# An emission planner with new costs, a margin for background row products, and bias tables loaded in three pieces

## The chip, the cores and the metric

The kernel runs on one core of one Trainium2 chip. The metric is the device time of one execution in microseconds; 1758.64 us is the median of three runs of the kernel before. The core's engines are TensorE (PE: matrix multiplies and transposes; PEld: the loading of its weights), VectorE (DVE), ScalarE (ACT), GpSimd (POOL) and SyncE (SP, which issues most transfers). Each runs its own queue of instructions in order and meets the others through semaphores.

## The reference

Two layers of a diffusion backbone, fp32, on 256 latent tokens and 256 context tokens of width 2048. What matters here, shortened:

```python
for i in range(2):
    shift, scale, gate = split(silu(c) @ ada_w[i] + ada_b[i], 3)        # modulation, 3 x 2048
    h = rms_norm(x, norm_g[i]) * (1 + scale) + shift
    if i == 0:
        y = na_ssd_mixer(h, hc, ...)      # hc: the context, modulated in the same way by c_ctx
    else:
        y = short_conv_mixer(h, ...)      # h @ w_in, gated convolution over 3 tokens, @ w_out
    x = x + gate * y

# in na_ssd_mixer: one projection h @ w_in (14400 columns), then
s_lat = einsum(q, k) * scale + bias       # 16 heads of 128; bias from the table rpb by (row, column) distance
s_lat = where(mask, s_lat, -inf)          # 16 columns' neighbourhood on a grid of 4 rows x 64
p = softmax(concat([s_lat, s_ctx]))
# beside them 32 state-space heads (8 groups), both directions; both parts @ w_out
```

## The kernel before

All matrix weights stream from HBM once, as tiles of 128 x 1024 fp32 (512 KB). Each is split into a high part (rounded to TensorE's fp32r format by ScalarE, line 420, `split`) and a low part (the fp32 tile minus the high part, by VectorE, line 427, `low_part`). A product is three passes: high by high, high by low, low by high. There are five raw buffers and three places for split weights (`w`), so the next weight's split waits until TensorE has left a place. `chunk` takes one split weight and issues its multiplies; `proj` runs over a column block. The first layer's 16 modulated row blocks are built in `ada_gen`; then come, block by block, q, k, gates, v, and the state-space inputs; then `w_out`, and the second layer.

Everything beside the weight products is written as generators: attention heads (`head_gen`), state-space groups (`group_gen`, `make_x`, `make_b`, `make_c`), norms of q and k (`kq_gen`), and the rest of the modulation as row products (`gemv_gen`): the gate of layer one and all of layer two, 128 tiles `adaT` of 128 x 1024, each multiplied by the broadcast vector `csb` and summed by one VectorE instruction (line 823, `gp`). A generator yields what it needs before its next step, as `W_(engine, tiles, nb)`, and the kernel writes out its instructions when the planner allows the step.

The planner (`Plan`) is a model of the chip that runs while the program is written. It keeps a clock per engine (`t`), the planned end of the last write (`w`) and the last read (`r`) of each tile part, and one DMA clock at 270 bytes a nanosecond. `add` books each emitted instruction with `cost`. After each few multiplies `pump` asks `may` for each waiting step, in three queues with horizons: `urgent` 4500 ns, `side` (heads and groups) 2500 ns, `back` (the row products only) 1500 ns. For VectorE and ScalarE the test is

```python
return t <= now + hor and rdy <= max(t, now) + 400     # line 270; now: PE's clock, t: the engine's
```

where `rdy` is the planned end of the writes that the step needs. For a step of TensorE in `back`, 4000 ns are added to `rdy`. So the planner sets no time on the chip: it sets only the order in which each engine's instructions stand in its queue. `force` writes out steps until a condition holds; line 1888 forces the row products of the second layer before its norm, line 1723 the last ones.

The attention bias of a head is a tile `bias` of 128 x 768, two of them in turn. Each head loads 672 columns of it (line 1073) with one transfer; the host builds the table with two gaps of 176 zeros between the parts that hold values (0 to 127, 304 to 367, 544 to 671). The mask is added to the three parts (line 1078), and the score step reads 2 x 208 columns, gaps included, for each half of the tokens (line 1096).

Of the kernel before, what the change touches and what calls it, by code (L numbers as in the profile page):

```python
# [37 lines left out]
class Plan:  # L38
# [5 lines left out]
    def __init__(self):  # L44
        self.t = dict.fromkeys(("PE", "DVE", "ACT", "POOL", "SP"), 0.0)
        self.w, self.r, self.last = defaultdict(float), defaultdict(float), defaultdict(float)
        self.dma = 0.0
        self.pool = (0.0, 0.0)

# [8 lines left out]
        hi = ap.offset + sum(abs(s) * (c - 1) for s, c in a)  # L58
        return [(n, u) for u in range(ap.offset // 256, hi // 256 + 1)]

    def ready(self, aps):
        return max((self.w[k] for a in aps for k in self.keys(a)), default=0.0)

    @staticmethod
    def size(a):
# [5 lines left out]
    def cost(self, e, op, i, ins, outs):  # L71
        n = max(self.size(a) for a in ins + outs)
        if e == "PE":
            n, cols = self.size(outs[0]), outs[0].ap[0][1]
            if i.is_transpose:
                return n / 1.2 + 3, 190
            if ins[0].dtype == F32R:
                return 9 + 0.434 * n, 190
            return 2 * max(55, n / 1.2) * (0.27 if cols == 32 else 0.52 if cols == 64 else 1) + (80 if cols < 128 else 0), 190
        if e == "DVE":  # L80
            if op == "Memset":
                return n * 0.26 + 60, 90
            if op in ("Reciprocal", "TensorReduce"):
                return n * 1.04 + 70, 90
            if len([a for a in ins if self.size(a) >= n]) >= 2 or op == "ISA" or self.psum(ins):
                return n * 1.22 + 70, 90
            return n * 0.6 + 130, 90
        if e == "ACT":
            return n * 0.85 + 150 + (200 if len(outs) > 1 else 0), 100
        if e == "POOL":  # L90
            return (n * 186 if n < 70 else n * 2.4) + 150, 60
        return 60, 0
# [5 lines left out]
    def add(self, b):  # L98
        i = b.ins
        e, op = self.NAMES[str(i.engine).split(".")[-1]], i.opcode  # L100
        ins = [x.bass_ap for x in i.ins if hasattr(x, "bass_ap")]
        outs = [x.bass_ap for x in i.outs if hasattr(x, "bass_ap")]
        ki, ko = [k for a in ins for k in self.keys(a)], [k for a in outs for k in self.keys(a)]
        s = self.t[e]
        for k in ki:
            s = max(s, self.w[k] + 60)
        for k in ko:
            s = max(s, 0.0 if e == "PE" else self.w[k] + 60, self.r[k] + 60)
        if op == "DMACopy":
            n = 4  # L110
            for _, c in outs[0].ap:
                n *= c
            self.t[e] = s + 450
            if e == "SP":
                self.dma = max(self.dma, s + 1000) + n / self.RATE
                done = free = self.dma + 1000
            else:
                done = free = max(self.dma, s + 1000) + n / self.RATE + 2500
        else:
            d, lat = self.cost(e, op, i, ins, outs)  # L120
            if e == "DVE" and not self.psum(ins + outs) and self.pool[0] <= s < self.pool[1]:
                s = self.pool[1]
            if e == "POOL":
                self.pool = (s, s + d)
            self.t[e] = s + d
            free, done = s + d, s + d + lat
        for k in ki:
            self.r[k] = max(self.r[k], free)
            self.last[k[0]] = max(self.last[k[0]], free)
        for k in ko:  # L130
            self.w[k] = done
            self.last[k[0]] = max(self.last[k[0]], done)
        return b

# [7 lines left out]
def kernel(ctx: ExitStack, tc, x, cx, ada0, w0, adaT, w_in, w_out, sc_in, sc_out, rpb, small, const,  # L142
# [7 lines left out]
    V, S, G, T, DMA = nc.vector, nc.scalar, nc.gpsimd, nc.tensor, nc.sync  # L150
    DMA2 = nc.scalar
    plan = Plan()
    E = plan.add

    def st(shape, tag, dt=F32, name=None):
        return sb.tile(list(shape), dt, tag=tag, name=name or tag, bufs=1)

    def drt(shape, name):
        return dr.tile(list(shape), F32, name="dram_" + name)
# [79 lines left out]
    def grow(task):  # L239
        _, t, h = task.cond  # L240
        if t - task.tmps > budget[0] or h - task.halves > budget[1]:
            return False
        cap(task, t, h)
        return True

    def may(task, hor, isurg):
        eng, aps, nb = task.cond
        if eng == "if":
            return aps()
        if eng == "grow":  # L250
            return grow(task)
        if nb and len(free_b) < nb + (0 if isurg else reserve[0]):
            return False
        if eng == "DVE":
            lows_try()
        now, t = plan.t["PE"], plan.t["ACT" if eng == "AQ" else eng]
        rdy = plan.ready(aps)
        if eng == "AQ":
            return t <= now + hor and rdy <= t
        if hor < 2000 and nb and sorted(plan.last[b.tensor.name] for b in free_b)[nb - 1] + 3000 > now:  # L260
            return False
        if hor < 2000:
            rdy += 4000 if eng == "PE" else 0
        if eng == "PE":
            if nb:
                rdy = max(rdy, sorted(plan.last[b.tensor.name] for b in free_b)[nb - 1])
            return rdy + (0 if isurg else 800) <= now + 100
        if eng == "SP":
            return rdy <= max(t, now) + 200
        return t <= now + hor and rdy <= max(t, now) + 400  # L270
# [7 lines left out]
    def pump():  # L278
        splits_try()
        again = True  # L280
        while again:
            again = False
            for q, hor in HOR[:2] if hold[0] else HOR:
                for task in list(q):
                    if not begin(task):
                        continue
                    if task.cond == "end":
                        sweep(q)
                        continue
                    if may(task, hor, q is urgent):  # L290
                        run(q, task)
                        if task.cond == "end":
                            sweep(q)
                        again = True
                        break
                if again:
                    break
# [134 lines left out]
    def lows_try():  # L432
        while lows and not hold[0] and plan.ready([lows[0][1]]) <= max(plan.t["PE"], plan.t["DVE"]) + 200:
            low_part()
# [340 lines left out]
    bias = [st([128, 3, 256], f"bias{k}") for k in range(2)]  # L775
# [149 lines left out]


    vd = drt([256, 512], "vd")
    dcol = P_("dcol")


# [136 lines left out]
    def head_gen(a, h):  # L1067
        hd = 4 * a + h
# [1 line left out]
        yield when(lambda: hd < 2 or ("pv", hd - 2) in got)  # L1070
        yield W_("SP")
        bf = bt.rearrange("p a b -> p (a b)")[:, :672]
        E(DMA.dma_start(bf, rpb[hd]))
        yield W_("DVE", bt)
        for o_, m_ in ((0, mask[:, 0:32]), (304, mid), (544, mask[:, 32:64])):
            n_ = m_.shape[-1]
# [77 lines left out]
        for i, (kt, vt, q_) in enumerate(BLOCKS):  # L1154
# [8 lines left out]
                          op=ALU.mult))  # L1163
# [388 lines left out]
    for h in range(4):  # L1552
        spawn(side, head_gen(0, h))
# [11 lines left out]
    def do_qk(a, nxt):  # L1565
        psQ = banks(2)
        proj(512, "act", psQ, 4)
        spawn(urgent, kq_gen("Q", a, psQ, 2, statq, QT, QL, True), 2)
        psK = banks(4)
        proj(512, "act", psK, nxt)  # L1570
        spawn(urgent, kq_gen("K", a, psK, 4, statk, KT, KL, True), 4)
        for h in range(4 if a < 3 else 0):
            spawn(side, head_gen(a, h))
# [19 lines left out]
    for h in range(4):  # L1593
        spawn(side, head_gen(3, h))
# [31 lines left out]
    done = []  # L1626
# [484 lines left out]
```

## Time and profile before

| | |
|---|---|
| median of 3 runs | 1758.64 us (1757.49 to 1760.16) |
| the profiled execution | 1761.34 us, of which the span of its instructions 1759.6 us |
| busy TensorE / VectorE / ScalarE | 1733.2 / 1218.6 / 768.1 us |
| mean granted TensorE clock | 0.999 |
| moved by DMA | 381.86 MB, 217 GB/s in the mean |

In the rows shown below, `L427` is line 427 of the kernel; `bank<-hH,w` names the tile written and the tiles read; a bracket `[0.77 <-DVE w L427]` is the idle time of the engine just before the instruction and what ended it. Rows of the timeline begin with the start in us from the span's start and the duration in us. `DVE raw L823 <- DMA raw<-in_adaT: 23.0, 24, 2.8` in the waits means: line 823 on VectorE waited for that transfer, 23.0 us in total, 24 times, 2.8 at most. In the table by stage each row is a stretch of time: its length, busy time and instruction count of each engine, the granted clock as a share of full speed, the busy share of the DMA engines, and GB/s. A transfer's row has its count, KB each, and the median us from issue to landing. TensorE's ends are modelled, so its busy time is not its peak rate.

### The profile page before, as it was taken

To read this page: it belongs to the slowest core of one execution; us is meant where nothing else is said; L and a number is where in the kernel's file an instruction comes from. 1 tells how busy PE (TensorE), PEld (TensorE's weight loads), DVE (VectorE), ACT (ScalarE), POOL (GpSimd) and SP (SyncE) were. 2 spreads that over 40 slices of the span, in tenths; PEclk is the share of its full clock that TensorE was granted. 3 is DMA by queue.
4 is the path that set the end of the run, shared out by engine and by line. 5 is a ranking of instruction groups with operands and counts; after the bars stand their busy time and mean duration, and the time that the engine had idled before them with its cause. 6 is when DMAs were issued, how large, how long until landed. Compare 5 with 4: busy or idle time off the path is not lost.

```text
span 1759.6 us, 25036 instructions
## 1 busy us (share of the span) xinstructions
PE 1733.2 (99%) x9451; PEld 1462.6 (83%) x9451; DVE 1218.6 (69%) x2042; ACT 768.1 (44%) x1330; POOL 31.4 (2%) x26
## 2 busy tenths in 40 slices
PE   6999999999999999999999999999999999999998
PEld 4777989888888888888888898888888888888887
DVE  5666777878476868676878687887668555555554
ACT  5333544446243436243436343664445444444432
POOL 0000100000000001000000000000000000000000
PEclk9999999999999999999999999999999999999999
DMA  9977644685765766665677567767867666666563
GB/s 368 347 295 258 206 150 150 201 241 190 231 198 158 239 190 209 207 220 171 212 219 219 180 213 239 242 227 266 290 218 251 208 187 192 191 191 191 190 205 120
DMA packets 188761, 381.86 MB, mean 217 GB/s; under 512 B 15536, under 2 KB 51168, under 8 KB 188640
## 3 DMA queue, kind: packets, MB, share of 16 engines
q1 hardware_dynamic: 181376, 373.68, 65.4%
q10 hardware_dynamic: 7264, 6.58, 1.1%
q8 instruction: 74, 1.21, 0.3%
q14 instruction: 47, 0.39, 0.1%
HBM read 372.71 MB, written 7.50 MB: 216 GB/s over the span
## 4 chain that ended last, share of the span: by engine, by line
PE 94%; DMA 2%; DVE 2%; ACT 1%; issue 0%; SPq 0%; POOL 0%; DVEq 0%; ACTq 0%
PE bank L195 90%; PE bank L199 3%; DMA tmp<-dram_csr 1%; DVE w L427 1%; DMA raw<-in_adaT 1%; DMA raw<-in_ada 0%; DVE raw L823 0%; DMA bias<-in_rpb 0%; ACT w L420 0%; DVE tmp L1456 0%; ACT tmp L1441 0%; DVE tmp L1445 0%; SPq L583 0%; ACT tmp L1451 0%; DVE tmp L759 0%
## 5 line engine op out<-in xcount | busy, mean ns | idle before, releaser
L420 ACT CAST w<-raw 128x1024 fp32r<-128x1024 f32 x343 | 359.1, 1049 | 519.9 <-PE bank L195 443.6
L427 DVE TENSOR_TENSOR w<-raw,w 128x1024 fp32r<-128x1024 f32 x343 | 416.5, 1218 | 232.9 <-ACT w L420 223.6
L195 PE MATMUL bank<-hH,w 128*128 128x256 f32 (+1 forms) x2064 | 488.4, 325 | 5.4 <-DVE w L427 5.4
L195 PE MATMUL bank<-w,hH 128*128 128x512 f32 x1280 | 406.3, 395 | 2.7 <-ACT hH L757 2.5
L195 PEld LDWEIGHTS bank<-hH,w 128*128 128x128 f32 x2064 | 345.7, 189 | 38.4 <-DVE w L427 6.6
L195 PE MATMUL bank<-hL,w 128*128 128x256 f32 (+1 forms) x1040 | 335.0, 322 | 0.0
L195 PEld LDWEIGHTS bank<-w,hH 128*128 128x128 f32 x1280 | 236.8, 188 | 54.1 <-issue 3.9
L195 PE MATMUL bank<-w,hL 128*128 128x512 f32 x640 | 249.5, 390 | 0.1
L195 PEld LDWEIGHTS bank<-hL,w 128*128 128x128 f32 x1040 | 197.0, 189 | 14.4
L195 PE MATMUL bank<-w,h 128*128 128x512 f32 x768 | 179.7, 390 | 0.0
L823 DVE CUSTOM_DVE_ANT_0 raw<-raw,csb 128x1024 f32<-128x1024 f32 x128 | 155.6, 1220 | 28.7 <-DMA raw<-in_adaT 23.0
L195 PEld LDWEIGHTS bank<-w,h 128*128 128x128 f32 x768 | 143.6, 188 | 29.6
L195 PEld LDWEIGHTS bank<-w,hL 128*128 128x128 f32 x640 | 120.1, 188 | 25.5 <-DVE hL L763 0.6
L195 PE MATMUL bank<-w,mix 128*128 128x512 f32 x588 | 138.6, 392 | 0.8 <-DVE w L427 0.8
L195 PEld LDWEIGHTS bank<-w,mix 128*128 128x128 f32 x588 | 109.3, 188 | 23.5 <-DVE w L427 1.7
L1276 DVE SCALAR_TENSOR_TENSOR tmp<-bank,cwh,tmp 128x508 f32<-128x508 f32 (+1 forms) x96 | 71.2, 745 | 1.8
L195 PE MATMUL bank<-KL,h 128*128 128x512 f32 x264 | 63.8, 389 | 0.0
L427 DVE TENSOR_TENSOR KL<-raw,KL 128x1024 fp32r<-128x1024 f32 x32 | 39.2, 1224 | 32.4 <-ACT KL L420 32.4
L427 DVE TENSOR_TENSOR QL<-raw,QT 128x1024 fp32r<-128x1024 f32 x32 | 39.2, 1224 | 29.4 <-ACT QT L420 29.3
L427 DVE TENSOR_TENSOR wL<-raw,wH 128x1024 fp32r<-128x1024 f32 x31 | 37.9, 1224 | 30.4 <-ACT wH L420 30.4
L195 PEld LDWEIGHTS bank<-KL,h 128*128 128x128 f32 x264 | 49.5, 188 | 10.2
L195 PE MATMUL bank<-QT,h 128*128 128x512 f32 x168 | 56.2, 391 | 0.0
(292 smaller groups left out, 1972.6 us busy)
## 6 DMA issues: line engine op xcount, KB each, us to landing
raw<-in_w_in SPq DMA_DIRECT2D x196, 512.0 KB, 3.8
raw<-in_adaT SPq DMA_DIRECT2D x128, 512.0 KB, 4.7
raw<-in_sc_in SPq DMA_DIRECT2D x128, 512.0 KB, 3.7
raw<-in_w_out SPq DMA_DIRECT2D x64, 512.0 KB, 4.9
raw<-in_ada SPq DMA_DIRECT2D x34, 512.0 KB, 6.7
raw<-in_sc_out SPq DMA_DIRECT2D x32, 512.0 KB, 3.6
PT<-in_ada SPq DMA_DIRECT2D x16, 512.0 KB, 6.9
raw<-in_w SPq DMA_DIRECT2D x16, 512.0 KB, 6.2
```

Of the source, the lines that this page charges most:

```text
L195: E(T.matmul(o, l, r, start=start, stop=stop, skip_group_check=True))
L199: E(T.transpose(o, i, ident if k == 128 else ident[:k, :k]))
L420: E(S.copy(H, v))
L427: E(V.tensor_tensor(out=Lo, in0=v, in1=H.bitcast(F32), op=ALU.subtract))
L823: E(V.tensor_tensor_reduce(out=raw, in0=raw, in1=csb, scale=1.0, scalar=0.0, op0=ALU.mult, op1=ALU.add, accum_out=gp[:, h, m:m + 1]))
L1276: E(V.scalar_tensor_tensor(out=do, in0=di, scalar=cwh[:, 32 * k + ch:32 * k + ch + 1], in1=do, op0=ALU.mult, op1=ALU.add))
```

## The change

Three edits.

1. The host's bias table has no gaps any more (320 columns). The two bias tiles' columns 128 to 543 are zeroed once by GpSimd, and each head loads its three parts with three transfers.
2. For a VectorE step of the `back` queue 2000 ns are added to `rdy`.
3. The planner's model: new costs of VectorE and ScalarE, a new latency to other engines, and no wait between instructions of the same engine (the planner keeps which engine wrote and read a part last).

```diff
@@ class Plan
+        self.wby, self.rby = defaultdict(str), defaultdict(str)
...
-    def ready(self, aps):
-        return max((self.w[k] for a in aps for k in self.keys(a)), default=0.0)
+    def ready(self, aps, e=None):
+        return max((self.w[k] for a in aps for k in self.keys(a) if self.wby[k] != e), default=0.0)
...
@@ def cost
+        wide = len([a for a in ins if self.size(a) >= n])
         if e == "DVE":
             if op == "Memset":
-                return n * 0.26 + 60, 90
+                return n * 0.26 + 60, 120
             if op in ("Reciprocal", "TensorReduce"):
-                return n * 1.04 + 70, 90
-            if len([a for a in ins if self.size(a) >= n]) >= 2 or op == "ISA" or self.psum(ins):
-                return n * 1.22 + 70, 90
-            return n * 0.6 + 130, 90
+                return n * 1.04 + 190, 120
+            if wide >= 2 or op == "ISA" or self.psum(ins):
+                return n * 1.045 + (137 if op == "ISA" else 128 if op == "TensorScalarPtr" else 70), 120
+            return (n * 0.4 + 205 if n > 32 else 80), 120
         if e == "ACT":
-            return n * 0.85 + 150 + (200 if len(outs) > 1 else 0), 100
+            if op == "Activation":
+                d = n * 0.83 + (110 if self.psum(ins) else 190 if len(outs) > 1 else 105)
+                return (d if self.psum(ins) else max(d, 293)), 120
+            return (n * 0.83 + 55 if self.psum(ins) else n * 0.85 + 90), 120
...
@@ def add
         for k in ki:
-            s = max(s, self.w[k] + 60)
+            if self.wby[k] != e:
+                s = max(s, self.w[k] + 60)
         for k in ko:
-            s = max(s, 0.0 if e == "PE" else self.w[k] + 60, self.r[k] + 60)
+            if self.wby[k] != e:
+                s = max(s, self.w[k] + 60)
+            if self.rby[k] != e:
+                s = max(s, self.r[k] + 60)
...
+        if op == "DMACopy":
+            e = "DMA"
         for k in ki:
+            if free >= self.r[k]:
+                self.rby[k] = e
             self.r[k] = max(self.r[k], free)
...
         for k in ko:
-            self.w[k] = done
+            self.w[k], self.wby[k] = done, e
...
@@ def may
-        rdy = plan.ready(aps)
+        rdy = plan.ready(aps, eng)
...
         if hor < 2000:
-            rdy += 4000 if eng == "PE" else 0
+            rdy += 4000 if eng == "PE" else 2000 if eng == "DVE" else 0
...
@@ before the first heads
+    for b_ in bias:
+        E(G.memset(b_.rearrange("p a b -> p (a b)")[:, 128:544], 0.0))
...
@@ def head_gen
-        E(DMA.dma_start(bf, rpb[hd]))
+        for o_, c_, n_ in ((0, 0, 128), (304, 128, 64), (544, 192, 128)):
+            E(DMA.dma_start(bf[:, o_:o_ + n_], rpb[hd, :, c_:c_ + n_]))
...
@@ on the host
-    gap = np.zeros((16, 128, 176), np.float32)
-    table = np.concatenate([pick(0, kc[:32]), gap, pick(0, kc[32:40]), pick(1, kc[24:32]), gap, pick(1, kc[32:])], axis=2)
+    table = np.concatenate([pick(0, kc[:32]), pick(0, kc[32:40]), pick(1, kc[24:32]), pick(1, kc[32:])], axis=2)
```

In a row such as `n * 1.045 + 70, 120`, `n` is the number of columns, the first value the time in ns until the engine is free, the second the time after that until another engine can use the result.

## The prediction

> **What bounds the kernel now.** I read the page's first two parts, then the chain of waits, the table by stage, the waits of TensorE, and the timeline around each of its waits.
>
> ```profile
> span 1759.6 us, 25036 instructions
> PE 1733.2 (99%) x9451; PEld 1462.6 (83%) x9451; DVE 1218.6 (69%) x2042; ACT 768.1 (44%) x1330; POOL 31.4 (2%) x26
> ```
>
> TensorE is busy in 1733.2 of 1759.6 us. The change touches none of its instructions, only their order and what they wait for. So the change can gain at most TensorE's idle time and what its clock lost. The table by stage tells where that lies (columns: busy us and instruction count of PE, PEld, DVE, ACT, POOL; then the granted clock, DMA share, GB/s):
>
> ```profile
> 0.00:40.00 40.00, 25.25 (x189) 16.79 (x189) 22.82 (x69) 24.97 (x55) 2.41 (x8) 1.00 0.96 373
> 200.00:240.00 40.00, 40.00 (x313) 38.48 (x312) 34.10 (x49) 25.57 (x55) 5.46 (x2) 1.00 0.63 196
> 400.00:440.00 40.00, 38.35 (x296) 35.65 (x293) 35.85 (x82) 23.57 (x65) 4.40 (x3) 1.00 0.57 182
> 640.00:680.00 40.00, 38.32 (x242) 33.90 (x240) 28.26 (x63) 24.16 (x75) 0.00 (x0) 1.00 0.74 226
> 680.00:720.00 40.00, 37.91 (x225) 33.45 (x226) 34.41 (x75) 16.83 (x34) 6.14 (x3) 0.96 0.47 147
> 1120.00:1160.00 40.00, 39.22 (x204) 32.37 (x203) 33.95 (x71) 23.78 (x48) 0.70 (x1) 1.00 0.82 258
> 1720.00:1760.00 40.00, 34.59 (x153) 28.31 (x151) 15.61 (x17) 7.70 (x8) 0.00 (x0) 0.98 0.32 105
> ```
>
> The first row's 14.75 us idle are the first transfers and norms; the last row's 5 us are the last multiply, add and store. No edit aims at either. Between them, TensorE waits five times on the low part of a weight (line 427: the fp32 weight minus its rounded copy, on VectorE):
>
> ```profile
> PE bank L195 <- DVE w L427: 6.2, 5, 3.0
> 409.53 0.50 PE L195 MATMUL bank<-hH,w 128*128 128x256 f32 x2 [0.77 <-DVE w L427]
> 413.40 0.50 PE L195 MATMUL bank<-hH,w 128*128 128x256 f32 x2 [0.88 <-DVE w L427]
> 669.16 0.51 PE L195 MATMUL bank<-hH,w 128*128 128x256 f32 x2 [0.81 <-DVE w L427]
> 682.09 0.50 PE L195 MATMUL bank<-hH,w 128*128 128x256 f32 x2 [2.96 <-DVE w L427]
> 1152.85 2.11 PE L195 MATMUL bank<-w,mix 128*128 128x512 f32 x8 [0.78 <-DVE w L427]
> ```
>
> The longest wait costs twice: the stage that begins at 680 has a clock of 0.96, and 0.04 of 40 us is 1.6 us. The stage of the two waits near 410 kept 1.00. So 6.2 + 1.6 = 7.8 us are all that the interior can give, 0.44% of 1758.64. What had VectorE late is in its own rows:
>
> ```profile
> 407.70 0.63 DVE L1078 TENSOR_TENSOR bias<-bias,const 128x128 f32<-128x128 f32 x3 [0.24 <-DMA bias<-in_rpb]
> 410.11 1.23 DVE L823 CUSTOM_DVE_ANT_0 raw<-raw,csb 128x1024 f32<-128x1024 f32 x1 [0.64 <-DMA raw<-in_adaT]
> 666.74 1.23 DVE L823 CUSTOM_DVE_ANT_0 raw<-raw,csb 128x1024 f32<-128x1024 f32 x1 [0.23 <-DMA raw<-in_adaT]
> 675.98 0.63 DVE L1078 TENSOR_TENSOR bias<-bias,const 128x128 f32<-128x128 f32 x3 [1.15 <-DMA bias<-in_rpb]
> 679.59 1.23 DVE L823 CUSTOM_DVE_ANT_0 raw<-raw,csb 128x1024 f32<-128x1024 f32 x1 [2.09 <-DMA raw<-in_adaT]
> 680.82 3.50 DVE L427 TENSOR_TENSOR w<-raw,w 128x1024 fp32r<-128x1024 f32 x3
> 1148.57 1.22 DVE L823 CUSTOM_DVE_ANT_0 raw<-raw,csb 128x1024 f32<-128x1024 f32 x1
> ```
>
> VectorE runs in order. Its queue stood still for a bias load (line 1078) or a row product's load (line 823), and the low parts behind, which needed neither, came late. At 1148.57 nothing was late; the product only stood ahead of the low parts.
>
> **The change part by part: the margin.** The row products are the only queue of the lowest rank, so the 2000 ns act on them alone: a product is put on VectorE's queue only when the plan has its data landed 1.6 us or more ago (2000 less the 400 of line 270) instead of up to 0.4 us ahead.
>
> ```profile
> DVE raw L823 <- DMA raw<-in_adaT: 23.0, 24, 2.8
> raw<-in_adaT SPq DMA_DIRECT2D x128, 512.0 KB, 4.7
> 672.92 6.64 DMA raw<-in_adaT
> ```
>
> The plan's time for 512 KB is 1000 + 524288/270 + 1000 = 3.94 us with an empty queue. Measured are 4.7 median and 6.64 in the bad place. Work that comes first by 2 us covers all but the longest of the 24 waits. At the three places where such a wait reached TensorE, 0.64 + 0.23 + 2.09 = 2.96 us go. Of the wait of 2.96 at 682.09 then about 0.87 stays, like the gaps near 410 that left the clock alone, so the 1.6 us go too: **-4.6 us**. Bounds: 0 (the queue meets another late load instead) and -6.2 (all but the wait at 1152.85 and the bias wait at 409.53, clock included). A product that waits longer also holds its raw buffer longer and ends later. The second layer needs the first 96 products:
>
> ```profile
> L823 DVE CUSTOM_DVE_ANT_0 raw<-raw,csb x128: 1212/1219/1227, 169.7 to 1366.8; 128x1024 f32<-128x1024 f32 x128
> 920.00:960.00 40.00, 8.61 (x14) 1.00 0.82 245
> 1308.13 0.56 POOL r L1715
> ```
>
> Summed over the table by stage of line 823 alone (two instructions a product), 90 are done by 920 us and the seven of this row hold the 96th; the norm that needs them stands at 1308 in the chain. These 350 us hide the delay; were they gone, the forced wait of line 1888 would show it, up to 2 us.
>
> **The bias in pieces.** Sixteen loads of 336 KB become 48, of 64, 32 and 64 KB: 2.8 MB less, 32 issues more.
>
> ```profile
> bias<-in_rpb SPq DMA_DIRECT2D x16, 336.0 KB, 4.7
> half<-in_strict SPq DMA_DIRECT2D x1, 128.0 KB, 3.5
> half<-in_rows SPq DMA_DIRECT2D x1, 64.0 KB, 3.3
> 669.56 0.94 SPq L1073 DMA_DIRECT2D bias<-in_rpb  x2
> 672.92 1.47 SPq L381 DMA_DIRECT2D raw<-in_adaT  x2
> ```
>
> Two heads' loads took 0.94 us of SP's queue, so 0.47 each; six take 2.8 at that price, 1.9 more. What stands behind them in that queue, two adaT loads here, moves by that. Against it stand 2 x 176 KB less, 0.97 us at the 373 GB/s of the first stage. Small loads here landed in 3.3 to 3.5 us, not in proportion to their size. So the last piece comes between 1.2 us sooner (3.5 for 4.7) and 0.9 later (1.9 less 0.97). The one TensorE wait that a bias load alone made is 0.77. I take 0, as the two ends straddle it; -0.8 to +1.8 (two such pairs) go into the range.
> [...] The rows above, where 64 KB and 128 KB cost nearly the same, agree with a fixed cost, but issues that overlap do not add it three times.
>
> The two GpSimd memsets of the gaps (416 columns) cost nothing on the path:
>
> ```profile
> 36.22 0.55 POOL L572 TENSOR_TENSOR rx<-rx,const 128x1 f32<-128x1 f32 x1 [5.81 <-DVE rx L571]
> 201.81 3.81 POOL L572 TENSOR_TENSOR statk<-statk,const 128x16 f32<-128x16 f32 x1 [165.04 <-DVE statk L571]
> ```
>
> They fall into 165 us in which GpSimd waits. Even at the power's own pace, 3.81 us for 16 columns, both take 198 us: 33 too many, which I count as excluded, since a memset does no power. If they slow VectorE beside them, TensorE was full there from 40 us on.
>
> **The plan's costs.** The plan charged a 1024-column subtraction 1.22 x 1024 + 70 = 1319 ns; it will charge 1140. Three back to back took 3.50 us (row at 680.82), the last one's 1.22 inside, so they follow each other at 1.14: the new figure is right and the old one 16% high. Between dependent instructions of one engine the plan allowed 150 ns and now none:
>
> ```profile
> 404.84 0.42 DVE L1480 TENSOR_TENSOR half<-bank,yi 128x256 f32<-128x256 f32 x1
> 405.30 0.43 DVE L1483 TENSOR_TENSOR half<-half,sz 128x256 f32<-128x256 f32 x1
> 399.84 0.43 DVE L1461 TENSOR_TENSOR tmp<-tmp 128x256 f32<-128x256 f32 x1
> 400.19 0.61 DVE L1445 SCALAR_TENSOR_TENSOR tmp<-tmp,csl 128x128 f32<-128x128 f32 x2
> ```
>
> The dependent pair starts 0.46 apart, the independent one 0.35: the truth is 0.11, nearer to the old value. The whole order of emission changes with these numbers, and nothing in the trace of before shows the new order. It can at best remove the rest, 7.8 - 4.6 = 3.2 us; at worst it does what the first rival says. I take -0.9, half of what the margin leaves at 413.40, 682.09 and 1152.85 (0.24 + 0.87 + 0.78 = 1.9).
>
> **Sum.** -4.6 + 0 - 0.9 = -5.5 us. The profiled execution took 1761.34 (span and 1.74 around it), 2.7 above the median; it becomes 1755.8, and the median 1758.64 becomes 1753.1. All interior waits gone would be 1750.8.
>
> **The rivals.** First, slower: *the lost reserve*. An urgent or side task goes onto VectorE's queue while the plan has it at most 4500 or 2500 ns ahead. With costs 16% high, 4.5 planned us were 3.9 real ones; now they are 4.5, so up to 0.6 us more stands ahead of a low part, and TensorE's own steps are slotted in with less reserve. VectorE has 33 us or more of work in nine of the 44 stretches of 40 us (from the one at 200 to the one at 1120, both above). Two low parts late by 0.6 in each are 9 x 2 x 0.6 = 10.8 us; less the 4.6, +6.2, so 1764.8. It decides from eight such waits on. For it: the five waits of before are all behind VectorE, and the 0.11 is now left out. Against it: the stretch at 200 had 34.10 us of VectorE and TensorE lost nothing.
>
> Second, *the next late load* (no change): ScalarE's wait for the decay rows takes the product's place, and the low part waits for its rounded copy.
>
> ```profile
> ACT tmp L1441 <- DMA tmp<-dram_csr: 19.9, 12, 2.9
> ```
>
> Its longest wait, 2.9, is as long as the one removed. Then -4.6 shrinks to some -2, 1756.6. For it: these loads stand in the same SP queue. Against it: none of TensorE's five waits shows it.
>
> [...]
>
> **How the numbers follow.** Forecast 0.48, lost reserve 0.32, next late load 0.12, late pieces 0.08. A measurement of this kernel tells about 0.2%, 3.5 us, from no change: faster means below 1755.1, slower above 1762.2. The forecast's own range is 1749 to 1756. Faster 0.48; the two middle rivals give no change, 0.20; slower 0.32. The range runs from 1748 (all waits gone, the bias gain of 0.8 and some of the start) to 1770 (28 late low parts instead of 18, 16.8 - 4.6 = +12); it leaves out the far end of the first rival, where a longer gap drops the clock again, and luckier starts.
>
> **What would show it.** Right: the wait of line 823 on adaT falls from 23.0 to a few us, no stage between 40 and 1300 has a clock under 1.00, and the five waits on line 427 shrink to under 2 us. Bias right: its last piece lands within 1 us of 4.7. Wrong: more than eight waits on line 427, or many short waits of TensorE on ScalarE or VectorE in the stretches with VectorE above 33 us; or products forced at the second layer's begin; or a start that is longer than 14.75 us of idle time.

## The result, and the profile after

| | before | after |
|---|---|---|
| median of 6 runs | 1760.26 us (1757.49 to 1762.73) | 1767.59 us (1767.16 to 1768.3) |
| the profiled execution | 1761.34 us, span 1759.6 | 1767.82 us, span 1766.0 |
| ratio after to before, 95% interval | | 1.0043 (1.003 to 1.0056) |

The change made the kernel 0.43% slower, 7.3 us by the medians. The page of the changed kernel:

```profile
span 1766.0 us, 25070 instructions
PE 1737.8 (98%) x9451; PEld 1464.1 (83%) x9451; DVE 1217.0 (69%) x2042; ACT 770.2 (44%) x1330; POOL 28.4 (2%) x28
```

In the changed source line 427 is line 440, line 1276 (the taps of the convolution before the state-space blocks) is 1292, line 823 is 836. (The last row products are forced at line 2023 of the kernel before, not at 1723.) The waits of TensorE, and those of VectorE on transfers, after the change:

```profile
PE bank L208 <- DVE w L440: 4.1, 9, 0.8
PE bank L212 <- DVE tmp L1299: 1.4, 3, 0.5
PE bank L208 <- DMA half<-in_strict: 0.9, 1, 0.9
PE bank L208 <- ACT w L433: 0.8, 1, 0.8
PE bank L212 <- DVE csl L1256: 0.4, 1, 0.4
DVE raw L836 <- DMA raw<-in_adaT: 10.6, 13, 2.1
```

Most of what was aimed at is gone: the row products wait 10.6 us for their loads instead of 23.0, no wait of 2.96 us is left and no stage between the start and the end has a clock under 1.00; VectorE's waits on the bias are no longer in the list. In their place stand more and shorter waits: nine behind low parts, up to 0.8 us (three of them under 0.2), and more of TensorE's own steps on VectorE's results (line 1299 ends a convolution, 1256 copies the decay sums). From 200 us on there are 18 waits of TensorE where there were six. The table by stage shows them spread over the first layer:

```profile
200.00:240.00 40.00, 38.48 (x293) 36.62 (x292) 31.34 (x59) 25.29 (x58) 4.52 (x2) 1.00 0.60 178
240.00:280.00 40.00, 38.41 (x216) 33.00 (x215) 36.46 (x86) 15.86 (x31) 0.00 (x0) 1.00 0.50 151
280.00:320.00 40.00, 39.27 (x256) 35.33 (x254) 29.54 (x47) 17.49 (x25) 0.00 (x0) 1.00 0.46 141
560.00:600.00 40.00, 39.24 (x269) 35.57 (x268) 33.17 (x46) 17.68 (x24) 0.00 (x0) 1.00 0.56 167
680.00:720.00 40.00, 40.00 (x268) 36.88 (x268) 33.10 (x69) 18.19 (x31) 3.59 (x2) 1.00 0.67 211
840.00:880.00 40.00, 39.20 (x257) 34.81 (x257) 35.88 (x53) 19.10 (x25) 0.00 (x0) 1.00 0.64 192
1000.00:1040.00 40.00, 39.23 (x247) 35.25 (x246) 27.62 (x35) 14.77 (x19) 0.00 (x0) 1.00 0.55 168
```

Three of these stages, at 560, 840 and 1000, lose the same 0.76 to 0.80 us, and in each the same thing happens. First VectorE's timeline of before, then that of after, then TensorE after:

```profile
563.07 1.23 DVE L427 TENSOR_TENSOR w<-raw,w 128x1024 fp32r<-128x1024 f32 x1 [2.42 <-ACT w L420]
564.22 5.32 DVE L1276 SCALAR_TENSOR_TENSOR tmp<-bank,cwh,tmp 128x508 f32<-128x508 f32 x7
569.45 1.22 DVE L427 TENSOR_TENSOR w<-raw,w 128x1024 fp32r<-128x1024 f32 x1
```

```profile
570.97 1.22 DVE L440 TENSOR_TENSOR w<-raw,w 128x1024 fp32r<-128x1024 f32 x1 [2.02 <-ACT w L433]
572.11 6.09 DVE L1292 SCALAR_TENSOR_TENSOR tmp<-bank,cwh,tmp 128x508 f32<-128x508 f32 x8
578.12 1.22 DVE L440 TENSOR_TENSOR w<-raw,w 128x1024 fp32r<-128x1024 f32 x1
```

```profile
577.92 0.40 PE L208 MATMUL bank<-hH,w 128*128 128x256 f32 x2
578.16 0.28 PE L208 MATMUL bank<-hL,w 128*128 128x256 f32 x1
578.28 0.40 PE L208 MATMUL bank<-hH,w 128*128 128x256 f32 x2
578.51 0.28 PE L208 MATMUL bank<-hL,w 128*128 128x256 f32 x1
579.39 0.39 PE L208 MATMUL bank<-hH,w 128*128 128x256 f32 x1 [0.60 <-DVE w L440]
```

Before, seven taps stood between two low parts; after, eight do, and the eighth takes 6.09 - 5.32 = 0.77 us. TensorE's work lasted through seven, not through eight. The last row also says what a wait costs: from the start of an hL row to the next hH row 0.12 us pass (578.16 to 578.28), but this time 0.88 (578.51 to 579.39). So 0.76 us are lost where the idle column says 0.60, because the hL row's modelled end, 0.28 after its start, counts as work. That is one reason why the page can show 4.6 us more *busy* TensorE (1737.8 for 1733.2) for the same 9451 matmuls: the busy time holds a part of each wait. At 0.16 us each, the twelve waits more make some 2 us of the 4.6; where the rest stands, the idle column does not say.

### The profile page after: what moved, and what is told of

The parts are those of the page before. It is cut to its first block, busy times and chain, and to the rows that moved or that the text cites. A ratio compares the mean times of both kernels' runs of the same rounds, so it can differ in the third digit from the quotient of the medians.

```text
span 1766.0 us, 25070 instructions
## 1 busy us (share of the span) xinstructions
PE 1737.8 (98%) x9451; PEld 1464.1 (83%) x9451; DVE 1217.0 (69%) x2042; ACT 770.2 (44%) x1330; POOL 28.4 (2%) x28
## 4 chain that ended last, share of the span: by engine, by line
PE 89%; DVE 7%; DMA 2%; ACT 1%; issue 1%; SPq 0%; POOL 0%; DVEq 0%; ACTq 0%
PE bank L208 86%; PE bank L212 3%; DVE w L440 2%; DVE tmp L1292 2%; ACT w L433 1%; DMA raw<-in_ada 0%; DMA tmp<-dram_csr 0%; ACT tmp L995 0%; DVE raw L836 0%; DVE tmp L1299 0%; DMA half<-in_rows 0%; DVE half L1292 0%; DMA bias<-in_rpb 0%; DMA raw<-in_w_in 0%; DVE tmp L1226 0%
## 5 line engine op out<-in xcount | busy, mean ns | idle before, releaser
L836 DVE CUSTOM_DVE_ANT_0 raw<-raw,csb 128x1024 f32<-128x1024 f32 x128 | 154.8, 1218 | 10.8 <-DMA raw<-in_adaT 10.6
```

What stands on the lines that cost most here:

```text
L836: E(V.tensor_tensor_reduce(out=raw, in0=raw, in1=csb, scale=1.0, scalar=0.0, op0=ALU.mult, op1=ALU.add, accum_out=gp[:, h, m:m + 1]))
```

## The experiments

Numbers with a ratio are against the kernel before on the same chip.

**Each edit alone, and the two loads' edits together.**

```diff
e1: kernel before; may():  rdy += 4000 if eng == "PE" else 2000 if eng == "DVE" else 0
e2: kernel before; host table without gaps, two memsets, three loads a head
e3: kernel after, without the lines of e1 and e2 (the plan alone)
e4: kernel before, with the lines of e1 and e2 (no new plan)
```

> The kernel before with the margin alone. Theory A (the new costs made the loss, because a queue's horizon now holds more real work ahead of the low parts; the margin by itself removes the waits behind late row products): -4.6 us against before, the wait of the row products on adaT down from 23.0 us to under 8, no clock drop. Theory B (the pieces of the bias made the loss): the same here. Theory C (any new order loses the tuned one's luck, whichever edit makes it): +3 to +8 us, with new short waits behind low parts. A margin that is itself the cause: +7.

Measured: 1759.33 us, ratio 0.9992 (0.9984 to 1.0001), no change. The waits on adaT did fall, to 8.6 us, but VectorE then stood before the bias load that used to come just ahead of the late product (timeline of VectorE):

```profile
671.92 0.63 DVE L1078 TENSOR_TENSOR bias<-bias,const 128x128 f32<-128x128 f32 x3 [4.62 <-DMA bias<-in_rpb]
...
673.31 3.49 DVE L427 TENSOR_TENSOR w<-raw,w 128x1024 fp32r<-128x1024 f32 x3
```

and on TensorE

```profile
674.58 0.50 PE L195 MATMUL bank<-hH,w 128*128 128x256 f32 x2 [1.91 <-DVE w L427]
```

The wait of 2.96 us became one of 1.91. Theory A missed this, and C too.

> The kernel before with the bias in pieces alone. Theory A: within 2 us of before, either way, the wait near 680 us and its clock drop still there. Theory B: +5 us or more, with VectorE waiting longer than 3.1 us in total for the bias. Theory C: +3 to +8 us.

Measured: 1765.15 us, ratio 1.0031 (1.002 to 1.0042). The mirror image: TensorE waits 6.0 us for three low parts, 2.8 at most, and now both stages have a lower clock (the table by stage):

```profile
400.00:440.00 40.00, 37.20 (x279) 35.07 (x275) 29.52 (x64) 21.99 (x64) 4.50 (x2) 0.96 0.57 171
680.00:720.00 40.00, 37.25 (x231) 33.04 (x230) 33.85 (x74) 18.02 (x35) 6.15 (x3) 0.96 0.49 151
```

VectorE waited 5.1 us in total for the bias instead of 3.1, as theory B asked for, and 26.0 for adaT. Whether the pieces or the new order made the first of these two gaps longer is not settled by this run.

> The kernel before with the plan's new costs and no wait inside one engine, alone. Theory A: +8 to +12 us, because the new short waits (some 13 us in the changed kernel) stand here beside some of the old ones behind late row products (up to 7.8 us with the clock). Theory B: 0 to -3 us. Theory C: +3 to +8 us.

Measured: 1767.15 us, ratio 1.0041 (1.0027 to 1.0055): the plan alone is as slow as the whole change. The bursts of eight taps are there, with the same waits of 0.60 us. Of theory A this confirms the short waits, not the sum: VectorE's waits on adaT rose to 41.6 us, 38 times, yet none of them reached TensorE for long: its waits behind low parts were 0.7 us at most.

> The kernel before with the margin and the bias in pieces, so the changed kernel without the new plan. Theory A: -4 to -6 us against before, some 12 us below the changed kernel. Theory B: +2 us or more. Theory C: +3 to +8 us.

Measured: **1752.75 us, ratio 0.9963 (0.9949 to 0.9976)**, the fastest kernel of this study, faster than both. After the first 90 us no wait is left in TensorE's whole list:

```profile
PE bank L195 <- DMA raw<-in_ada: 11.1, 1, 11.1
PE bank L195 <- ACT hH L757: 2.5, 2, 1.4
PE bank L199 <- ACT half L724: 1.0, 2, 0.5
PE bank L199 <- ACT x L613: 0.3, 1, 0.3
PE bank L195 <- DVE gt L789: 0.2, 1, 0.2
```

So in this order the margin and the pieces together gave what neither gave alone, and the new plan turned that into a loss of 1767.59 - 1752.75 = 14.8 us. On top of the kernel before, the plan alone cost 1767.15 - 1759.54 = 7.6 us, and beside the new plan the two edits gave nothing (1767.59 with them, 1767.15 without).

**What in the plan.**

```diff
e5: add():  same engine:  + elif e != "PE": s = max(s, self.w[k] - 10)      # 110 ns after the end
e6: add(), may():  the old waits inside an engine, new costs
e7: cost():  the old costs, no wait inside an engine
e8: HOR = ((urgent, 3500.0), (side, 2100.0), (back, 1200.0))
```

> The changed kernel, with 110 ns in the plan between dependent instructions of VectorE or of ScalarE, as the trace shows. Theory X (a horizon of 4500 planned ns holds more real work now, in the taps of the convolution above all, which are planned 0.66 us apart and run 0.77 apart): partly better, 1758 to 1763, since a tap is planned at 0.77 then and six instead of seven go into a horizon. Theory Y (the missing delay alone makes the loss): 1752 to 1756. Theory Z (the new costs' order is worse by accident, and any further change draws again): anywhere from 1753 to 1770, with waits in other places than before.

Measured: 1769.74 us, ratio 1.0062 (1.0046 to 1.0078). Not better; eight taps still stand in a row in the three blocks after the first, and the other waits moved to the norms of k and q (2.3 us behind line 1008) and to a state-space step (2.0 us behind line 1510). Theories X and Y are both wrong here.

> The changed kernel with the old waits inside one engine, so of the plan the new costs and latencies alone. Theory X: 1755 to 1760; a tap is planned at 0.659 + 0.18 = 0.84 again, so the bursts of eight taps are gone, while independent work is still planned tighter. Theory Y: 1752 to 1756. Theory Z: 1753 to 1770.

Measured: 1760.39 us, ratio 1.0007 (0.9998 to 1.0017). Just above X's range: 7.2 us of the 14.8 are back, seven taps stand in a row in the three blocks after the first, no wait behind them.

> The changed kernel with the old costs, so of the plan the missing delay alone. Theory X: 1756 to 1762; a tap is planned at 0.69, between the old 0.84 and the new 0.66, so most of the bursts stay. Theory Y: 1765 or more, as slow as the changed kernel. Theory Z: 1753 to 1770.

Measured: 1764.72 us, ratio 1.0034 (1.002 to 1.0047), outside X's range, just under Y's. Eight taps in a row in all four blocks, with a wait of 0.60 us behind each; besides, at a wait of 2.0 us near 1150 the clock of the stage from 1120 dropped to 0.91. So in these two orders neither the costs nor the missing delay alone makes the whole loss: each takes away a part of what the old plan charged too much.

> The changed kernel with shorter horizons in the same plan: 3500, 2100 and 1200 ns for 4500, 2500 and 1500. Theory X: 1752 to 1758, because five taps at most go ahead of a low part, as before. Theory Y: no change, 1765 or more. Theory Z: 1753 to 1770.

Measured: 1773.58 us, ratio 1.0084 (1.0069 to 1.0099). X is wrong as a cure. The taps obeyed (seven in a row, the waits of 0.60 gone), but TensorE's steps now came before their inputs more often:

```profile
PE bank L212 <- DVE tmp L1299: 3.1, 8, 0.5
PE bank L212 <- POOL r L1519: 2.5, 1, 2.5
PE bank L208 <- DVE w L440: 2.5, 5, 1.2
PE bank L212 <- DVE tmp L1004: 2.3, 4, 1.4
PE bank L208 <- DVE half L1506: 1.6, 2, 1.0
```

This led to theory R: the old plan's excess was a reserve in two places, in how much work a horizon lets ahead of a low part, and in how early a step of TensorE is slotted in. By this theory a shorter horizon mends the first and leaves the second.

**Reserve put back, one place or both.**

```diff
e9:  may():  return rdy + (500 if isurg else 1300) <= now + 100        # was 0 and 800; TensorE's steps
e10: add():  + if e in ("DVE", "ACT"): d *= 1.16                       # new costs, 16% too high
e11: e4 with RATE = 255.0                                              # was 270; bytes a ns of the plan's DMA
```

> The changed kernel, with 500 ns more between a planned result and the TensorE step that uses it (in the urgent and side queues). Theory R (the old costs' excess was a reserve in two places: VectorE bursts ahead of low parts, about 6.7 us of TensorE's excess in the changed kernel, and TensorE's own steps slotted in too early, about 5.8 us): 1760 to 1763, the waits of TensorE on conv outputs, norms and decay rows gone, those on low parts left. Theory Z (the new order is worse by accident): anywhere from 1753 to 1770, with waits of both kinds.

Measured: 1763.35 us, ratio 1.0017 (1.0008 to 1.0027), 4.2 us better than the changed kernel, 0.35 beyond R's range. As R says, the low parts' waits stayed and those of TensorE's steps shrank:

```profile
PE bank L208 <- DVE w L440: 4.2, 10, 0.8
PE bank L212 <- DVE tmp L1299: 0.8, 1, 0.8
PE bank L208 <- DVE half L1506: 0.5, 1, 0.5
```

> The changed kernel, with every duration of VectorE and ScalarE in the plan multiplied by 1.16, still without a wait inside one engine. Theory R: 1753 to 1760, since the reserve is back, whatever formula gives it. Theory Z: 1753 to 1770. If accuracy of the costs were what counts: 1768 or more.

Measured: 1755.71 us, ratio 0.9973 (0.9961 to 0.9984), 11.9 us better than the changed kernel by one multiplication that makes the plan less exact. Seven taps again in the three blocks after the first, and no wait behind them:

```profile
566.08 5.31 DVE L1294 SCALAR_TENSOR_TENSOR tmp<-bank,cwh,tmp 128x508 f32<-128x508 f32 x7
571.30 1.22 DVE L442 TENSOR_TENSOR w<-raw,w 128x1024 fp32r<-128x1024 f32 x1
```

> The kernel with the margin and the bias in pieces and the old plan, but the plan's DMA rate 255 bytes a ns for 270: a small change of the order of emission that is meant for nothing. Theory R: 1751 to 1756, as its reserve is untouched. Theory Z: up to 10 us above 1752.75, because that order was a lucky one.

Measured: 1767.01 us, ratio 1.0034 (1.0021 to 1.0047): 14 us slower than e4, so R was wrong here, and Z still too small. Two long waits came, one at 413 us behind low parts, ahead of which VectorE had stood 1.5 us for a bias load, and one at the border of the layers, where the next weight's cast stood behind the norm's activations in ScalarE's queue:

```profile
PE bank L195 <- ACT wH L420: 4.1, 1, 4.1
PE bank L195 <- DVE w L427: 3.3, 3, 2.0
```

**Is the loss the costs' or one order's?** A change of the rate in the changed kernel, the overcharged one and the old plan. It draws the order again, but not blindly: at 255 the plan has loads land later than at 270, at 285 sooner.

```diff
e12: kernel after, RATE = 255.0      e15: kernel after, RATE = 285.0
e13: e10, RATE = 255.0               e14: e4, RATE = 285.0
```

> The changed kernel with the plan's DMA rate 255 for 270, an order drawn again. Theory R (the short waits are made by the missing reserve, whatever the order): 1764 to 1772, with the waits behind eight taps at every state-space block again. Theory Z (the first draw was unlucky): below 1760 as likely as not, and the pattern gone.

Measured: 1784.44 us, ratio 1.0146 (1.0127 to 1.0165): more than R allowed, since the border's wait of 4.1 us and two lower clocks (0.96 in the stage from 680, 0.91 in the one from 1320, together 0.13 x 40 = 5.2 us) came on top of the short waits, all of which are there.

> The changed kernel with durations times 1.16 and the rate 255. Theory R: 1753 to 1760, few short waits, though a single long wait at the border of the layers may come as it did with the old plan at this rate. Theory Z: up to 1768.

Measured: 1756.94 us, ratio 0.9987 (0.9978 to 0.9997), inside R's range, though inside Z's too; the long wait at the border did not come.

> The old plan with the margin and the bias in pieces, at the rate 285. Theory R: 1752 to 1760, no series of short waits; at most one or two long ones, which come with the order. Theory Z: anywhere from 1752 to 1770.

Measured: 1765.32 us, ratio 1.0037 (1.0025 to 1.0049), above R's range. No series of short waits, but one load of the bias came 6.6 us late, TensorE lost 3.9 behind it, and the clock of the stage from 400 dropped to 0.91:

```profile
DVE bias L1081 <- DMA bias<-in_rpb: 9.0, 4, 6.6
PE bank L195 <- DVE w L427: 5.1, 2, 3.9
```

> The changed kernel at the rate 285. Theory R: 1764 to 1772 with the taps' waits at every block. Theory Z: anywhere from 1753 to 1770.

Measured: 1773.32 us, ratio 1.0083 (1.0064 to 1.0101), with the taps' waits at every block; 1.3 above R's range.

At three rates the new plan took 1767.6, 1784.4 and 1773.3 us, the old plan with the same loads 1752.8, 1767.0 and 1765.3, the overcharged one at two of them 1755.7 and 1756.9. So both hold: another rate moves the time of one plan by up to 17 us (in e12 one long wait and the clock make more than half of that), and at each rate the new plan is 8 to 17 us behind. The short waits behind the taps come with the number of taps: in the three blocks after the first, the seven kernels with eight taps in a row (after, e3, e5, e7, e9, e12, e15) have the wait of 0.60 us (once 0.61) in all 21 places; the ten with seven have none of it. In the first block this rule does not hold: e6 has eight taps there and no such wait, e10 eight and one of 0.34 us, e5 seven and one of 0.71. Three waits that cost 0.76 us each are also only 2.3 of the 14.8 us; the rest stands in the other waits and in the intervals that the idle column does not show.

## Why the prediction was wrong

The change was forecast to gain 5.5 us and cost 7.3. For the margin and the pieces together 4.6 were forecast and 6.8 measured (e4), though not in the way foreseen; what failed above all is the term for the plan.

**What bounds the kernel: right.** The differences that the traces show are waits of TensorE and its clock. The ceiling of 7.8 us held by the medians: e4, with no wait left in the interior, gained 6.8 against the 1759.54 of the kernel before beside it. It was not a strict one. Between the two profiled executions the span fell by 9.4 us (1759.6 to 1750.2), of which 3.0 are busy time (1733.2 to 1730.2), which the prediction took for work that no edit can touch.

**The margin, -4.6: right in kind, wrong as a term of its own.** Alone it gave nothing measurable (e1). The step that failed is that a wait of 2.96 us, of which 2.09 stood before the product, would shrink to 0.87. The bias load ahead of it in VectorE's queue was late too, and in e1's order it became late by 4.62, so that 1.91 us of the wait stayed. I had the second rival, a next late load, but named the decay rows for it. In the trace the next one stood a line above: the 1.15 us at 675.98.

**The bias in pieces, 0: the price alone is positive, its worth beside the margin is the rest.** Alone +5.6 us (e2), outside its bounds of -0.8 to +1.8. A second clock drop, which I had tied to the margin's wait only, is 1.6 us of it; where the rest stands is open, as the profiled execution, 1762.43, is the fastest of e2's seven. With the margin the pieces were 6.6 us better than the margin alone (e4 against e1). My reading is that two late loads in a row on one queue are one wait, so that taking away either leaves the other; at the rates 255 and 285 a bias load came late in spite of both edits (1.5 us in e11, 6.6 in e14). Each piece landed about 1 us sooner after its own issue than the 4.7 of before (transfers of the changed kernel, then the tile's view):

```profile
bias<-in_rpb SPq DMA_DIRECT2D x32, 64.0 KB, 3.7
bias<-in_rpb SPq DMA_DIRECT2D x16, 32.0 KB, 3.6
```

```profile
L942 POOL MEMSET bias<- x2: 446/446/447, 37.8 to 38.2; 128x416 f32 x2
```

But the third load is issued some 0.95 us after the first, so a head's last piece lands 4.6 us after its first issue, in the median, for 4.7 before: the 0 was right for the landing. The three loads of a head overlap: one after another they would take some 11 us (3.7 + 3.6 + 3.7, an estimate from the two rows), not 4.6. 64 KB and 32 KB landed alike, in 3.7 and 3.6 us. Late pieces, to which I had given 0.08, did not come in the changed kernel. The memsets took 0.45 us each in GpSimd's pause, as counted.

**The plan, -0.9: the step that failed.** It measured +14.8 us beside the margin and the pieces (after against e4), +7.6 alone (e3). I took half of a possible gain for an effect whose bad end I had worked out to +10.8 in the first rival, on the ground that the new cost of a low part is right. It is right, and a plan with costs 16% too high was still 11.9 us faster (e10). My first rival had the mechanism: the horizon of 4500 planned ns holds one more tap (4500/840 is 5.4 taps in the old plan, 4500/659 is 6.8 in the new), and the eighth is the 0.77 us. The count alone does not decide it: a tap is planned at 0.77 us in e5 and at 0.76 in e10, 5.9 taps in both, and e5 has eight in a row, e10 seven. The rival also named the second place, TensorE's steps slotted in with less reserve, without a price; in the one order of e9 it is worth 4.2 us. That the rival's 1764.8 came near to 1767.59 is in part luck: it counted 18 low parts late by 0.6 us and nine came, 4.1 us in total, and the 4.6 us that it took off for the margin were not gained beside the new plan. Its sign, more than eight waits on the low parts, did come true. Its counter-argument, that the stretch from 200 with 34.10 us of VectorE had lost nothing, was read from the old order; after the change that stretch loses 1.52 us. Putting back the 0.11 us between dependent instructions that I measured and the plan leaves out did not help (e5).

What is still open: how the 14.8 us divide among costs, latency and missing delay, since each partial plan (e6, e7) draws its own order, and one draw is worth up to 17 us; whether 16% is a reserve that holds in other orders than the two tried; and why the first block's burst of eight is harmless in e6.

## What to carry to other kernels

Where a cost model sets a static order, its excess can be slack that absorbs late results, and taking it out can cost more than the exactness gains. What helped here was to charge 16% too much, and another rate hardly moved that kernel (1755.71 to 1756.94 us); an explicit reserve for TensorE's steps alone gave 4.2 us (e9), and shorter horizons made it slower (e8). Look at what stands before a late load in the same queue: when it is late too, mending one of the two may only uncover the other (in e1 a wait of 2.96 us became one of 1.91). And judge a change of order on more than one draw, by the series of equal waits that stays and not by the time of one.

## What the hardware showed unexpectedly

The three waits of TensorE behind eight taps cost some 0.16 us more each than the idle column says (0.76 lost for 0.60 idle), so that a part of the loss stands in the page as busy time.

The granted clock fell on gaps of under 3 us. Besides the wait of 2.96 us before the change, those of 2.81 and 2.75 us in e2 took their stages to 0.96, and in e7 one of 1.99 us, followed at once by one of 0.47, took its stage to 0.91; a single one of 1.91 us (e1) or 2.0 us (e11) left its stage at 1.00, as did one of 2.5 us in e8 (the stage from 1120) and the nine of up to 0.8 us after the change. The length of a gap does not decide it, though: two stages fell to 0.96 with gaps of 1.37 and 0.27 us (e8) and of 0.93 and 0.27 us (e12), both before transposes of the norms of k and q (the rows of e8, then of e12).

```profile
400.00:440.00 40.00, 38.36 (x294) 36.16 (x293) 31.41 (x74) 20.69 (x60) 4.29 (x3) 0.96 0.58 176
680.00:720.00 40.00, 38.80 (x265) 36.39 (x264) 32.73 (x71) 18.73 (x38) 4.75 (x2) 0.96 0.67 195
```

In finer stretches the trace of before has the clock at 0.50 from 683.48 to 686.90, so for 3.4 us; in a stretch of the same length just before, from 680.06, TensorE was busy for 1.39; the other 2.03 are the end of the gap of 2.96. What besides the gaps decides when the clock falls stays open.
